# A hybrid gated-attention layer: three pairs of 256-column products made 512 columns wide, and the output's first product moved behind the last gate

## The chip, the cores and the metric

The kernel runs on one core of a Trainium2 chip. The metric is the device time of one execution in microseconds (us). Before the change the median of three runs is 765.3 us (764.86 to 766.08).

## The reference

One pre-norm layer on x of 1024 frames by 1024 columns, all float32:

```
h     = rmsnorm(x, norm_w)
parts = h @ w_in + b_in          # 1024 columns in; q, f, i, z of HGRN2; q, k, v, a, z of GLA; q, k, v, i, f, o, z of mLSTM
y_hg  = gated_head_norm(HGRN2(q, f, i), z)                # 4 heads, keys 128, values 128
y_gla = gated_head_norm(GLA(q, k, v, a), z)               # 4 heads, keys 64, values 128
y_ml  = gated_head_norm(mLSTM(silu(conv(q, k)), v, i, f) * sigmoid(o), z)   # 4 heads, keys 64, values 128
x     = x + concat(y_hg, y_gla, y_ml) @ w_out             # 1536 x 1024
out   = rmsnorm(x, final_norm_w)
```

Each branch is causal and worked out in chunks, with a state carried from one to the next. `gated_head_norm` normalises each head and multiplies by silu(z).

## The kernel before

**Products in three parts.** A float32 operand is split into a high and a low part of a shorter format (`whi`, `wlo` of weights; `HI[k]`, `LO[k]`, sixteen tiles named hT, of the normalised input, transposed). Each product of a block is three matmuls: high by high, high by low, low by high. `load_w` (L215 to 226) loads a raw weight tile of 128x1024 (`wraw`, two buffers, on SyncE's DMA queue), ScalarE copies the high part (L225), VectorE subtracts (L226). `whi` and `wlo` have three buffers each.

**Pieces.** The input projection is cut into pieces. An "nt" piece (`proj_nt`) holds 128 output columns as rows: two halves of 24 matmuls with 512 tokens. A "tn" piece (`proj_tn`, L354 to 376) holds tokens as rows: eight chunks of 128 tokens, each of 24 matmuls of 256 columns (L371 to 373), whose bank (`pm`, two in all) is then evacuated with scale and bias (`scaled`, L378). Tn pieces are the values of HGRN2 (v0, v1), of GLA (gv0, gv1), of mLSTM (mv0, mv1) and mLSTM's output gate (mo0, mo1); a tn piece of 256 columns holds two weight tiles.

**Order.** TensorE's order is that of the program text: `Weave` runs the pieces (`projections`, L908) as the main line and puts steps of attention chains between their triplets, by planned costs (0.65 for a triplet of 512 columns, 0.32 for one of 256), lags and free banks of PSUM (tags `pt`, `tp`, `po`, two banks each). The other engines' instructions are ordered by a scheduler, each engine in order; an instruction waits for its operands and buffers, and what stands behind it waits too. The order of the pieces in the last parts is, for r = 0 and 1: gq, gk, gv, two gz; then mq, mk, mv, mo, two mz.

**mLSTM's chain** (`ml_chain`, L806): convolution and silu of q and k (`conv`, L725 to 731), weights and attention matrices (`ml_att`, products L710, VectorE L711), states (`ml_states`), outputs (`ml_out`, L780). `ml_out` takes for each chunk a `po` bank, two or four small matmuls (L788, L790), and on ScalarE and VectorE the denominator (L792 to 794) and the gated output `osb` (L796), whose last read frees the bank. Then the head norm: squares on ScalarE (L525), the reciprocal root on GpSimd (`rstd_of`, L211 and L212), scaling (L528), transposes on TensorE (L533), the multiplication by silu(z) (L835).

**Sums.** `sum_steps` (L970 to 981) makes four sums of blocks of w_out for the output, through the two `wraw` buffers and back to DRAM, three steps each, between pieces.

**Output.** Behind all pieces seven products of 1536/2 x 512 blocks (a scheme that saves one of eight) of 72 matmuls each stand in program order (`product`, L1058 to 1068). The A operands are made of the y tiles by `a_form` (ScalarE L1040, VectorE L1041) after differences (`s2`, L1050 to 1052; `s1`, L1057), into hT tiles; the B operands by `b_form` (L1027 to 1029). y rows of HGRN2 and GLA are read back from DRAM. Product 1 (A11 by wq0) accumulates in four banks, is copied to P1 (L1117), and product 2 goes on adding in the same banks.

Of the kernel before, what the change touches and what calls it, by code (L numbers as in the profile page):

```python
# [45 lines left out]
PIECES = piece_columns()  # L46
WIDX, BIDX, VIDX = {}, {}, {}
NW = 0
for _n, _k, _c in PIECES:
# [82 lines left out]
def kernel(ctx: ExitStack, tc: tile.TileContext, x, xt, wt, wide, cols, vbias, wa2, wq, fw, masks, sel,  # L132
# [775 lines left out]
    def projections():  # L908
# [88 lines left out]

    with tc.manual_schedule(engines={mybir.EngineType.PE}):
        w.run(projections())

        nc.sync.dma_start(fwb, bass.AP(tensor=fw.tensor, offset=fw.offset, ap=[[0, 128], [1, D]]))
        for i in (0, 1, 2, 3):
            y_tile(i)
        for kh in range(2):
            for i in range(6):  # L1010
# [234 lines left out]
```

## Time and profile before

| | us |
|---|---|
| median of 3 runs | 765.3 (764.86 to 766.08) |
| profiled execution | 765.59 |
| its span on the core | 763.7 |
| TensorE busy | 747.7 (98%) |
| VectorE busy | 470.2 (62%) |
| ScalarE busy | 351.5 (46%) |
| GpSimd busy | 80.2 (11%) |

The mean granted clock of TensorE was 0.995 of full speed. The span runs from the first to the last instruction on the core; what lies around it is 1.9 us. Matmuls are pipelined, so a row of the trace overlaps the next, and the busy time is an upper bound on the work: how often matmuls start is read from the timeline. TensorE is the engine that sets the time; idle time on the others costs nothing in itself.

### The profile page before, as it was taken

The page shows a single profiled execution, that of the slowest core. Times are in us where ns is not written, and L with a number is a line of the kernel's source. Part 1 is how long each engine was busy: PE and PEld are TensorE (multiplying, and loading weights), DVE is VectorE, ACT ScalarE, POOL GpSimd, SP SyncE. Part 2 cuts the span into 40 slices and gives each one's busy share as a digit, 9 for nine tenths or more (in the row PEclk, how much of TensorE's full clock was granted, in tenths as well). Part 3 has the DMA queues.
Part 4 walks back from the last instruction along what each step waited for, and adds up shares of the span by engine and source line. Part 5 has one row for each costly group of instructions (what it writes and reads, how often), then busy time and mean ns, then how long its engine had stood idle before and what let it go on. Part 6 is the DMA issues. An engine that isn't in the chain of part 4 may idle for free.

```text
span 763.7 us, 14518 instructions
## 1 busy us (share of the span) xinstructions
PE 747.7 (98%) x5901; PEld 646.7 (85%) x5901; DVE 470.2 (62%) x998; ACT 351.5 (46%) x770; POOL 80.2 (11%) x107
## 2 busy tenths in 40 slices
PE   8999998999999999999999999999999999999996
PEld 6888886899887898788988889998899988878885
DVE  6896768676458447524753384543466258799863
ACT  6652669643453330554042661355252467264533
POOL 2000120010010020012000400001000112600011
PEclk9999999999999999999999999999999999999998
DMA  8331563031554041302021120122202067543323
GB/s 304 122 114 58 193 218 111 29 125 51 193 166 139 28 138 61 115 29 86 28 64 56 39 73 3 61 63 70 70 27 92 15 215 267 161 142 111 98 108 125
DMA packets 29826, 79.55 MB, mean 104 GB/s; under 512 B 3568, under 2 KB 7152, under 8 KB 29760
## 3 DMA queue, kind: packets, MB, share of 16 engines
q1 hardware_dynamic: 29088, 78.11, 31.0%
q8 instruction: 46, 0.75, 0.4%
q0 software_dynamic: 672, 0.53, 0.3%
q14 instruction: 20, 0.16, 0.1%
HBM read 62.69 MB, written 15.93 MB: 103 GB/s over the span
## 4 chain that ended last, share of the span: by engine, by line
PE 85%; DVE 6%; DMA 4%; ACT 2%; issue 2%; SPq 0%; POOL 0%; POOLq 0%; ACTq 0%; DVEq 0%
PE pm L339 11%; PE pm L341 11%; PE pm L340 11%; PE pm L371 8%; PE pm L372 8%; PE pm L373 8%; PE po L574 2%; PE po L576 2%; PE pt L489 2%; PE pt L559 1%; PE tp L533 1%; PE pt L458 1%; DMA wraw<-in_wt_dram 1%; PE tp L1067 1%; PE tp L1066 1%
## 5 line engine op out<-in xcount | busy, mean ns | idle before, releaser
L339 PE MATMUL pm<-hT,whi 128*128 128x512 f32 x400 | 163.0, 408 | 0.0
L341 PE MATMUL pm<-hT,wlo 128*128 128x512 f32 x400 | 157.1, 393 | 0.0
L340 PE MATMUL pm<-hT,whi 128*128 128x512 f32 x400 | 156.7, 392 | 0.0
L371 PE MATMUL pm<-whi,hT 128*128 128x256 f32 (+1 forms) x488 | 142.7, 292 | 0.0
L372 PE MATMUL pm<-wlo,hT 128*128 128x256 f32 (+1 forms) x488 | 138.4, 284 | 0.0
L373 PE MATMUL pm<-whi,hT 128*128 128x256 f32 (+1 forms) x488 | 138.3, 283 | 0.0
L371 PEld LDWEIGHTS pm<-whi,hT 128*128 128x128 f32 x488 | 93.2, 191 | 3.1 <-issue 2.2
L225 ACT ACTIVATE whi<-wraw 128x1024 fp32r<-128x1024 f32 (+4 forms) x47 | 45.6, 972 | 105.5 <-PE pm L373 55.8
L372 PEld LDWEIGHTS pm<-wlo,hT 128*128 128x128 f32 x488 | 93.3, 191 | 0.3
L373 PEld LDWEIGHTS pm<-whi,hT 128*128 128x128 f32 x488 | 93.2, 191 | 0.0
L341 PEld LDWEIGHTS pm<-hT,wlo 128*128 128x128 f32 x400 | 75.4, 188 | 16.6
L339 PEld LDWEIGHTS pm<-hT,whi 128*128 128x128 f32 x400 | 75.7, 189 | 16.2 <-issue 1.5
L340 PEld LDWEIGHTS pm<-hT,whi 128*128 128x128 f32 x400 | 75.8, 189 | 13.6
L226 DVE TENSOR_TENSOR wlo<-wraw,whi 128x1024 fp32r<-128x1024 f32 (+4 forms) x47 | 52.4, 1117 | 27.3 <-ACT whi L225 27.2
L378 DVE SCALAR_TENSOR_TENSOR big<-pm,rs,vb 128x256 f32<-128x256 f32 x72 | 32.2, 455 | 49.2 <-PE pm L373 49.1
L399 POOL COPY zg<-zg 128x1 f32<-128x1 f32 x12 | 21.7, 1810 | 219.2 <-ACT zg L397 219.2
L500 ACT ACTIVATE att<-dc 32x128 f32<-32x128 f32 (+1 forms) x48 | 16.5, 344 | 49.2 <-DVE dc L480 48.7
L211 POOL TENSOR_SCALAR st<-st 128x4 f32<-128x4 f32 x24 | 5.0, 207 | 268.6 <-ACT sq L525 268.6
L351 DVE TENSOR_TENSOR f<-pm,RSB 128x512 f32<-128x512 f32 x18 | 12.4, 688 | 30.9 <-PE pm L341 30.8
L397 ACT ACTIVATE zg<-zg,pc 128x512 f32<-128x512 f32 x24 | 17.2, 719 | 29.5 <-DVE zg L351 29.4
L525 ACT ACTIVATE sq<-po 128x128 f32<-128x128 f32 x64 | 17.8, 278 | 27.7 <-PE po L581 23.2
L351 DVE TENSOR_TENSOR zg<-pm,RSB 128x512 f32<-128x512 f32 x22 | 15.2, 691 | 23.1 <-PE pm L341 22.8
(396 smaller groups left out, 1458.2 us busy)
## 6 DMA issues: line engine op xcount, KB each, us to landing
wraw<-in_wt_dram SPq DMA_DIRECT2D x39, 512.0 KB, 3.9
wraw<-in_wq_dram SPq DMA_DIRECT2D x27, 512.0 KB, 3.6
wraw<-wsum SPq DMA_DIRECT2D x18, 512.0 KB, 3.5
wsum<-wraw SPq DMA_DIRECT2D x12, 512.0 KB, 2.9
big<-ydram SPq DMA_DIRECT2D x18, 256.0 KB, 5.4
big<-in_xt_dram SPq DMA_DIRECT2D x5, 512.0 KB, 5.7
ydram<-zg SPq DMA_DIRECT2D x8, 256.5 KB, 2.4
ydram<-zg SPq DMA_DIRECT2D x8, 255.5 KB, 3.3
```

The costliest lines, as they stand in the source:

```text
L225: nc.scalar.activation(hi[:, s], raw[:, s], AF.Copy)
L226: nc.vector.tensor_sub(lo[:, s], raw[:, s], hi[:, s].bitcast(F32))
L339: nc.tensor.matmul(p, hi[:, ks], HI[k][:, s], start=k == 0, stop=False)
L340: nc.tensor.matmul(p, hi[:, ks], LO[k][:, s], start=False, stop=False)
L341: nc.tensor.matmul(p, lo[:, ks], HI[k][:, s], start=False, stop=k == KC - 1)
L351: nc.vector.tensor_mul(dst(half), p, RSB[:, s])
L371: nc.tensor.matmul(p, HI[k][:, ts], hi[:, ks], start=k == 0, stop=False)
L372: nc.tensor.matmul(p, HI[k][:, ts], lo[:, ks], start=False, stop=False)
L373: nc.tensor.matmul(p, LO[k][:, ts], hi[:, ks], start=False, stop=k == KC - 1)
L378: nc.vector.scalar_tensor_tensor(dst, p, rs[:, c:c + 1], b, op0=OP.mult, op1=OP.add)
L399: nc.gpsimd.tensor_copy(z[:, 0:1], z[:, T:T + 1])
L525: nc.scalar.activation(sq, o[:, j, :], AF.Square, accum_out=st[:, j:j + 1])
```

## The change

The values of both GLA halves (gv0 and gv1), and for each r mLSTM's values and output gate (mv, mo), become one piece of 512 columns (`proj_tn2`: eight chunks of 24 matmuls, planned at 0.68 a triplet). It holds four weight tiles, so `whi` and `wlo` get four buffers. gv1 is thus made at r = 0; in its place at r = 1 stands mq0's projection, which before stood behind all gz. The values of a pair count as done with the gate's fourth chunk, and `ml_states`' second half waits for all gates, so `ml_out` moves from the mo piece into the mz pieces.

The output's first product becomes a last piece (`out_first`), woven with what is left of mLSTM's chain: it takes over the hT tiles, reads y2 to y5 of the first quarter early into four small tiles, makes both operands, takes four `pm` banks in turn and copies each to P1 (two tiles named al). Product 2 starts its own banks, and P1 is added to the result on VectorE (four additions). L numbers of the changed kernel are other ones: L339 to 341 become L344 to 346, L788 and L790 become L818 and L820, L796 becomes L826, L1041 becomes L1065.

```diff
-            hilo = [wp.tile([128, 1024], F32R, name=nm, bufs=3) for nm in ("whi", "wlo")]
+            hilo = [wp.tile([128, 1024], F32R, name=nm, bufs=4) for nm in ("whi", "wlo")]
...
+    def proj_tn2(names, evac):
+        vb = wk.tile([128, 512], F32, name="vb", bufs=1)
...
+        w = [load_w(wt[WIDX[names[0]] + a]) for a in range(4)]
+        for c in range(NC):
+            p = pmain.tile([128, 512], F32, name="pm")
+            ts = slice(c * 128, (c + 1) * 128)
+            for k in range(KC):
+                hi, lo = w[k // 2]
+                ks = slice(512 * (k % 2), 512 * (k % 2) + 512)
+                nc.tensor.matmul(p, HI[k][:, ts], hi[:, ks], start=k == 0, stop=False)
+                nc.tensor.matmul(p, HI[k][:, ts], lo[:, ks], start=False, stop=False)
+                nc.tensor.matmul(p, LO[k][:, ts], hi[:, ks], start=False, stop=k == KC - 1)
+                yield 0.68
+            for a in range(2):
+                evac[a](c, p[:, 256 * a:256 * a + 256], vb[:, 256 * a:256 * a + 256])
...
         yield from ml_states(r, K, E, V, S, 0)
+        yield lambda: len(gates) == NC
         yield from ml_states(r, K, E, V, S, 1)
+        states_of.append(r)
...
-            vs.append((yield from proj_v(f"gv{r}")))
+            if r == 0:
+                vv = [v_tile() for _ in range(2)]
+                yield from proj_tn2(PAIRS[0], [ev for _, ev in vv])
+                for a in range(2):
+                    gvs[a].append(vv[a][0])
+            else:
+                pq0.append((yield from proj_conv("mq0")))
...
-            V = yield from proj_v(f"mv{r}")
+            V, ev_v = v_tile()
...
                 gts.append(c)
-            yield from proj_tn(f"mo{r}", evo)
+                if c == 3:
+                    Vs.append(V)
+            yield from proj_tn2(PAIRS[1 + r], [ev_v, evo])
             for a in range(2):
                 zs.append((yield from proj_z(f"mz{2 * r + a}")))
+        yield from out_first()
...
+    def out_first():
+        yield lambda: len(states_of) > 1
...
+        load_y(0)
+        load_y(1)
+        tmp = [wk.tile([128, 768], F32, name="qm")[:, 0:512] for _ in range(2)] + [junk, wk.tile([128, 512], F32, name="kd")]
+        for i in range(2, 6):
+            nc.sync.dma_start(tmp[i - 2], ydram[i, :, 0:512])
+        b = b_form(wq[0])
+        a = a_form(lambda i: A11(i) if i < 2 else tmp[i - 2])
+        for c in range(4):
+            p = pmain.tile([128, 512], F32, name="pm")
+            yield from product(c, p, a, b, True, True)
+            nc.scalar.activation(P1[c], p, AF.Copy)
...
-        b1, a1 = b_form(wq[0]), a_form(A11)
-        pa = banks(tags_a)
...
-        for c in range(4):
-            product(c, pa[c], a1, b1, True, False, blocks=range(4))
-        for c in range(4):
-            product(c, pa[c], a1, b1, True, False, blocks=range(4, 6))
-            nc.scalar.activation(P1[:, c], pa[c], AF.Copy)
-        a2, b2 = a_form(A12), b_form(wq[2])
         for c in range(4):
-            product(c, pa[c], a2, b2, False, True)
+            nc.vector.tensor_add(xs(c, L), P1[c], xs(c, L))
+            run(c, pa[c], a2, b2, True, True)
```

How instructions stand now. First TensorE where mLSTM's last outputs begin their second pair of banks; `pm` is the last gate projection, `po` the outputs' banks. Before:

```order
L339 MATMUL pm_6433<-hT_113,whi_6428 128x512
L340 MATMUL pm_6433<-hT_114,whi_6428 128x512
L341 MATMUL pm_6433<-hT_113,wlo_6429 128x512
L788 MATMUL po_6482<-big_5785,att_95 128x129 [waits DVE_49,Activation_49]
L790 MATMUL po_6482<-S_6098,big_5804 128x129
L788 MATMUL po_6482<-big_5785,att_95 128x129
L790 MATMUL po_6482<-S_6098,big_5804 128x129
```

After, the same step (`po_5965` is the third bank, `po_5934` the first, whose place it takes):

```order
L344 MATMUL pm_5919<-hT_109,whi_5869 128x512
L345 MATMUL pm_5919<-hT_110,whi_5869 128x512
L346 MATMUL pm_5919<-hT_109,wlo_5870 128x512
L344 MATMUL pm_5919<-hT_111,whi_5869 128x512
L345 MATMUL pm_5919<-hT_112,whi_5869 128x512
L346 MATMUL pm_5919<-hT_111,wlo_5870 128x512
L818 MATMUL po_5965<-big_5383,att_95 128x129 [waits DVE_49,Activation_49]
L820 MATMUL po_5965<-S_5599,big_5417 128x129
L818 MATMUL po_5965<-big_5383,att_95 128x129
L820 MATMUL po_5965<-S_5599,big_5417 128x129
```

In both a third bank comes nine matmuls behind the second; after the change this stands in mz3's second half, before in mz2.

VectorE at that place, before: `osb` from the two banks, with what stands ahead.

```order
L793 TENSOR_TENSOR dn_6456<-dn_6456,mcol_123 128x2 [waits Activation_49]
L794 RECIPROCAL dn_6456<-dn_6456 128x2 [waits DVE_49]
L796 SCALAR_TENSOR_TENSOR osb_6449<-po_6451,dn_6456,big_6079 128x128 [waits DVE_49,PE_49]
L796 SCALAR_TENSOR_TENSOR osb_6450<-po_6451,dn_6456,big_6079 128x128
L793 TENSOR_TENSOR dn_6467<-dn_6467,mcol_123 128x2 [waits Activation_49]
L794 RECIPROCAL dn_6467<-dn_6467 128x2 [waits DVE_49]
L796 SCALAR_TENSOR_TENSOR osb_6449<-po_6462,dn_6467,big_6079 128x128 [waits DVE_49,PE_49]
L796 SCALAR_TENSOR_TENSOR osb_6450<-po_6462,dn_6467,big_6079 128x128
L1029 TENSOR_TENSOR al_6691<-wraw_6711,al_6690 128x1024 [waits DMAHW7_49,Activation_49]
L793 TENSOR_TENSOR dn_6487<-dn_6487,mcol_123 128x2 [waits Activation_49]
```

After: the last rows ahead of the first bank's `osb` (`hT` and `big` are operands of the output's products; the twelve rows ahead of these are nine more of the kind, two of two columns, and one product by a gate).

```order
L1065 TENSOR_TENSOR hT_6017<-dc_89,hT_6016 128x512 [waits PE_49,Activation_49]
L1065 TENSOR_TENSOR hT_6017<-kd_6050,hT_6016 128x512 [waits DMAHW6_49,Activation_49]
L1075 TENSOR_TENSOR qm_6330<-big_6043 128x512 [waits DVE_49]
L1065 TENSOR_TENSOR hT_6019<-big_6038,hT_6018 128x512 [waits PE_49,Activation_49]
L1065 TENSOR_TENSOR hT_6019<-big_6043,hT_6018 128x512 [waits DMAHW2_49,Activation_49]
L824 RECIPROCAL dn_5939<-dn_5939 128x2 [waits DVE_49]
L824 RECIPROCAL dn_5950<-dn_5950 128x2 [waits DVE_49]
L1076 TENSOR_TENSOR big_6038<-big_6038,qm_6324 128x512 [waits DVE_49]
L1076 TENSOR_TENSOR big_6043<-big_6043,qm_6330 128x512 [waits DVE_49]
L826 SCALAR_TENSOR_TENSOR osb_5932<-po_5934,dn_5939,big_5385 128x128 [waits DVE_49]
L826 SCALAR_TENSOR_TENSOR osb_5933<-po_5934,dn_5939,big_5385 128x128
```

The evacuations of the first bank (`osb` from `po_5934`) now stand behind operations of the output's operands, which in before came later.

SyncE's queue after GLA's values: before, `wraw` loads of pieces (in_wt), of the sums (wsum, in_wq) and the sum's store.

```order
L224 DMA wraw_3346<-in_wt_dram 128x1024 [waits DMAHW6_49,DVE_49]
L977 DMA wraw_3527<-wsum_479 128x1024 [waits DMAHW7_49,DMAHW1_49,DVE_49]
L978 DMA wraw_3528<-in_wq_dram 128x1024 [waits DMAHW2_49,DMAHW0_49,DVE_49]
L980 DMA wsum_479<-wraw_3527 128x1024 [waits DMAHW3_49,DVE_49]
L224 DMA wraw_3534<-in_wt_dram 128x1024 [waits DMAHW2_49]
L977 DMA wraw_3643<-wsum_479 128x1024 [waits DMAHW3_49]
L518 DMA ydram_122<-zg_2486 128x511 [waits DVE_49]
L515 DMA ydram_122<-zg_2486 128x513 [waits DVE_49,Pool_49]
L978 DMA wraw_3644<-in_wq_dram 128x1024 [waits DMAHW4_49,DVE_49]
L358 DMA vb_3907<-in_vbias_dram 128x256 [waits DMAHW1_49,DVE_49]
L980 DMA wsum_479<-wraw_3643 128x1024 [waits DVE_49]
L224 DMA wraw_3653<-in_wt_dram 128x1024 [waits DMAHW0_49]
```

After:

```order
L548 DMA ydram_122<-zg_2486 128x511 [waits DVE_49]
L545 DMA ydram_122<-zg_2486 128x513 [waits DVE_49,Pool_49]
L1115 DMA qm_6049<-ydram_122 128x512 [waits DMAHW7_49,DMAHW6_49,PE_49]
L1019 DMA wraw_3589<-in_wq_dram 128x1024 [waits DMAHW4_49,DVE_49]
L387 DMA vb_4586<-in_vbias_dram 128x256 [waits DVE_49]
L387 DMA vb_4586<-in_vbias_dram 128x256 [waits DMAHW3_49]
L1021 DMA wsum_479<-wraw_3588 128x1024 [waits DVE_49]
L229 DMA wraw_3604<-in_wt_dram 128x1024 [waits DMAHW5_49,DMAHW1_49]
L1018 DMA wraw_3665<-wsum_479 128x1024 [waits DMAHW4_49]
L1019 DMA wraw_3666<-in_wq_dram 128x1024 [waits DMAHW5_49,DVE_49]
L1021 DMA wsum_479<-wraw_3665 128x1024 [waits DMAHW0_49,DVE_49]
L229 DMA wraw_3675<-in_wt_dram 128x1024 [waits DMAHW7_49]
```

In both, steps of the sums and loads of pieces alternate; after the change one sum stands whole ahead of the load for gz1 (wraw_3604), and another between it and the load for gq1 (wraw_3675).

## Rows read from the trace of the kernel before

**Rows 1.** The page's first part: busy us of each engine, share of the span, instructions
```profile
PE 747.7 (98%) x5901; PEld 646.7 (85%) x5901; DVE 470.2 (62%) x998; ACT 351.5 (46%) x770; POOL 80.2 (11%) x107
```

**Rows 2.** Waits of TensorE: for whom, us in total, times, longest us
```profile
PE pt L429 <- ACT al L699: 2.0, 1, 2.0
...
PE pt L1068 <- DVE hT L1041: 1.3, 1, 1.3
...
PE pm L1066 <- DVE zg L1160: 0.6, 1, 0.6
```

**Rows 3.** Timeline of TensorE, 603 to 640: start us, us, engine, line, operation, tiles, form
```profile
604.62 0.28 PE L371 MATMUL pm<-whi,hT 128*128 128x256 f32 x1
...
604.98 0.28 PE L371 MATMUL pm<-whi,hT 128*128 128x256 f32 x1
...
637.74 0.39 PE L339 MATMUL pm<-hT,whi 128*128 128x512 f32 x1
...
639.10 0.39 PE L1066 MATMUL po<-whi,hT 128*128 128x512 f32 x1
```

**Rows 4.** Timeline of TensorE, 616 to 635, around mLSTM's last outputs
```profile
618.27 0.38 PE L788 MATMUL po<-big,att 128*128 128x129 f32 x2
...
619.97 0.48 PE L339 MATMUL pm<-hT,whi 128*128 128x512 f32 x1
...
633.85 0.60 PE L533 MATMUL tp<-ident,osb 128*128 128x128 f32 x4
634.20 0.48 PE L339 MATMUL pm<-hT,whi 128*128 128x512 f32 x1
```

**Rows 5.** Timeline of VectorE, 612 to 645
```profile
616.16 0.61 DVE L796 SCALAR_TENSOR_TENSOR osb<-po,dn,big 128x128 f32<-128x128 f32 x2
...
621.96 0.23 DVE L793 TENSOR_TENSOR dn<-dn,mcol 128x2 f32<-128x2 f32 x2
...
636.89 0.69 DVE L1050 TENSOR_TENSOR big<-big 128x512 f32<-128x512 f32 x1
...
642.92 0.69 DVE L351 TENSOR_TENSOR zg<-pm,RSB 128x512 f32<-128x512 f32 x1
```

**Rows 6.** Stretches: busy us of each engine, granted clock (PEclk), DMA share, GB/s
```profile
120.00:122.00 2.00, 0.55 (x2) 0.19 (x1) 2.00 (x11) 1.82 (x2) 0.00 (x0) 1.00 0.92 272
124.00:126.00 2.00, 2.00 (x13) 1.59 (x7) 2.00 (x8) 1.97 (x4) 0.00 (x0) 0.63 0.15 20
126.00:128.00 2.00, 2.00 (x7) 1.57 (x6) 1.62 (x8) 1.97 (x3) 0.36 (x1) 0.52 0.64 242
```

**Rows 7.** Groups by line and shape: busy us, mean ns of one | idle before, releaser
```profile
L225 ACT ACTIVATE whi<-wraw 128x1024 fp32r<-128x1024 f32 x39 | 41.2, 1058 | 100.6 <-PE pm L373 55.8 <-PE pm L340 37.5 <-DMA wraw<-in_wt_dram 5.9
...
L226 DVE TENSOR_TENSOR wlo<-wraw,whi 128x1024 fp32r<-128x1024 f32 x39 | 47.6, 1223 | 27.1 <-ACT whi L225 27.0
...
L979 DVE TENSOR_TENSOR wraw<-wraw 128x1024 f32<-128x1024 f32 x12 | 14.7, 1225 | 10.1 <-DMA wraw<-in_wq_dram 9.2 <-issue 0.8
```

**Rows 8.** Groups of VectorE by line and shape, convolution and mLSTM preparation
```profile
L511 DVE SCALAR_TENSOR_TENSOR zg<-tp,pc,zg 128x512 f32<-128x512 f32 x16 | 11.7, 746 | 4.4 <-PE tp L533 4.3
...
L730 DVE SCALAR_TENSOR_TENSOR f<-f,pc 128x1024 f32<-128x1024 f32 x6 | 7.7, 1280 | 0.1
...
L815 DVE TENSOR_SCALAR big<-al 64x1024 f32<-64x1024 f32 x4 | 2.7, 685 | 1.2 <-ACT al L731 1.1
...
L728 DVE TENSOR_SCALAR f<-f,pc 128x1024 f32<-128x1024 f32 x2 | 1.6, 807 | 0.0
```

**Rows 9.** The page's DMA issues: count, KB each, median us from issue to landing
```profile
wraw<-in_wt_dram SPq DMA_DIRECT2D x39, 512.0 KB, 3.9
wraw<-in_wq_dram SPq DMA_DIRECT2D x27, 512.0 KB, 3.6
...
wsum<-wraw SPq DMA_DIRECT2D x12, 512.0 KB, 2.9
```

**Rows 10.** Timeline of GpSimd, 640 to 670
```profile
644.42 17.01 POOL L399 COPY zg<-zg 128x1 f32<-128x1 f32 x1 [12.43 <-ACT zg L397]
```

More of the change, by code (lines that the diff above doesn't have):

```diff
@@ L46 @@
 PIECES = piece_columns()
+PAIRS = (("gv0", "gv1"), ("mv0", "mo0"), ("mv1", "mo1"))
+PAIRED = {n for p in PAIRS for n in p}
 WIDX, BIDX, VIDX = {}, {}, {}
@@ L58 @@
         VIDX[_n] = len(VIDX)
+for _p in PAIRS:
+    WIDX[_p[0]] = NW
+    NW += 4
 NB = len(BIDX)
@@ L996, in y_tile, with b_form, a_form @@
         return Y[i]
+    ASET, BSET, P1, made = [], [], [], [0, 0]
+    def b_form(src):
+        t = BSET[made[1] % 2]
+        made[1] += 1
+        for i in range(3):
+            raw = wp.tile([128, 1024], F32, name="wraw", bufs=2)
+            nc.sync.dma_start(raw, src[i])
+            nc.scalar.activation(t[2 * i], raw, AF.Copy)
+            nc.vector.tensor_sub(t[2 * i + 1], raw, t[2 * i].bitcast(F32))
+        return t
+    def a_form(src):
+        t = ASET[made[0] % 2]
+        made[0] += 1
+        for i in range(6):
+            s = slice(512 * (i % 2), 512 * (i % 2) + 512)
+            raw = src(i)
+            hi, lo = t[i // 2 * 2][:, s], t[i // 2 * 2 + 1][:, s]
+            nc.scalar.activation(hi, raw, AF.Copy)
+            nc.vector.tensor_sub(lo, raw, hi.bitcast(F32))
+        return t
@@ new lines, in product @@
+    def product(c, p, a, b, first, last, cols=slice(0, 512)):
+        for i in range(6):
+            ahi, alo = (a[i // 2 * 2 + q][:, 512 * (i % 2) + 128 * c:512 * (i % 2) + 128 * c + 128] for q in range(2))
+            bs = slice(512 * (i % 2) + cols.start, 512 * (i % 2) + cols.stop)
+            bhi, blo = (b[i // 2 * 2 + q][:, bs] for q in range(2))
+            nc.tensor.matmul(p[:, cols], ahi, bhi, start=first and i == 0, stop=False, skip_group_check=True)
+            nc.tensor.matmul(p[:, cols], ahi, blo, start=False, stop=False, skip_group_check=True)
+            nc.tensor.matmul(p[:, cols], alo, bhi, start=False, stop=last and i == 5, skip_group_check=True)
+            yield 0.69
@@ L1015 @@
-        hts = [ht.tile([128, 1024], F32R, name="hT") for _ in range(16)]
-        w0 = [wp.tile([128, 1024], F32R, name=nm, bufs=3) for _ in range(3) for nm in ("whi", "wlo")]
-        w0[4:4] = [fp.tile([128, 1024], F32R, name="al", bufs=2) for _ in range(2)]
-        ASET = [hts[0:6], hts[6:12]]
-        BSET = [w0[0:6], hts[12:16] + w0[6:8]]
-        made = [0, 0]
-        def b_form(src):
-            t = BSET[made[1] % 2]
-            made[1] += 1
-            for i in range(3):
-                raw = wp.tile([128, 1024], F32, name="wraw", bufs=2)
-                nc.sync.dma_start(raw, src[i])
-                nc.scalar.activation(t[2 * i], raw, AF.Copy)
-                nc.vector.tensor_sub(t[2 * i + 1], raw, t[2 * i].bitcast(F32))
-            return t
@@ L1070 @@
-        stats = const.tile([128, NC, 8], F32, name="stats")
+        for i in range(2, 6):
+            load_y(i)
         U2 = [wk.tile([128, 512], F32, name=nm) for nm in ("osb", "osb", "kd", "kd")]
@@ L1127 @@
         for c in range(4):
-            product(c, pb[c], a6, b6, True, False)
-            nc.vector.tensor_sub(U2[c], P1[:, c], pb[c])
+            run(c, pb[c], a6, b6, True, False)
+            nc.vector.tensor_sub(U2[c], P1[c], pb[c])
         a7, b7 = a_form(A11), b_form(wsum[2])
@@ L1185, in _layout @@
         vb[VIDX[name], :256] = b_in[c:c + 256]
+        if name in PAIRED:
+            continue
         for a in range(2):
@@ L1188, in _layout @@
                 wt[i + a] = kmajor(w_in[512 * a:512 * a + 512, c:c + 256])
+    first = {n: c for n, _, c in PIECES}
+    for pair in PAIRS:
+        both = np.concatenate([w_in[:, first[n]:first[n] + 256] for n in pair], axis=1)
+        for a in range(4):
+            wt[WIDX[pair[0]] + a] = kmajor(both[256 * a:256 * a + 256])
     cols[:, PC_NW:PC_NW + KC] = f("norm_w")[0].reshape(KC, 128).T
```

114 lines of the change are left out of this document (55 added, 59 removed).

## The prediction

> **What bounds the kernel now.** I read the busy shares first: TensorE (PE) is busy 747.7 of 763.7 us, so only 16 us of its span is idle [rows 1]. Then its table of waits: they are short and few; the longest is 2.0 us, and of the two in the output projection one is 1.3 us and one 0.6 us [rows 2]. So the time is TensorE's stream of matmuls, and two things can change it: fewer or cheaper matmuls, or new waits. Then the timeline of TensorE for the price of a matmul. Rows overlap there (a row of 0.39 us starts 0.23 us after the one before), so a price is the distance between starts: 0.36 us for three matmuls of 256 columns, 1.36 us for six of 512 [rows 3], that is 0.120 and 0.227 us once medians are taken over many rows. Last I read the queues of VectorE (DVE), ScalarE (ACT) and the loads around the places where the order of the changed kernel puts a wait.
>
> **The pairs.** Six pieces of 192 matmuls of 256 columns become three of 192 of 512. Per pair 384 x 0.120 = 46.1 us become 192 x 0.227 = 43.6 us; three times 2.5 us is 7.5 us less, all on TensorE's path. Nothing is multiplied less: two columns in one matmul cost 0.95 of what they cost in two. A matmul of 512 columns with weights and tokens in these places is not in the trace; the nearest row is the 512-column one of [rows 3], and I take it (bounds: 7 to 8 us saved).
> The Trainium skill, "TensorE: Matmul & The Clock Gate", back-to-back issue gap, gives columns / 2.4 GHz plus 2.5 ns for a matmul alone, 109 and 216 ns, by which the three pairs would save an estimated 1.2 us and the whole sum be 6 us worse. The trace has 120 ns for the small one, so here it disagrees, and the measured distances stand.
>
> **The wait ahead of product 1 (the largest term).** ml_out's second half needs two "po" banks again after 9 matmuls, and they are freed by VectorE's L826. In the order of before only operations of two columns stand ahead of the same step (L796), and TensorE's row at 618.27 follows its matmul without a wait [rows 4]. Now 17 operations on 128x512 tiles in SBUF (L1065, L1074, L1075, L1076, L1081, one L867) stand there, the operands of products 1 and 6. The same kinds of operations start 6.03/10 = 0.603 us apart (ten between the row at 636.89 and the one at 642.92) [rows 5]. Count from the start of mz3's second half, t = 0. VectorE cannot begin earlier than 0.7, since the evacuation of the first half stands ahead; the first hT pair is free after three matmuls (0.68) and one ScalarE copy of 0.6, so it begins at 1.35. Then 17 x 0.603 = 10.25, four operations of two columns at 0.1, and two L826 at 0.3 [rows 5]: the bank is free at 12.6. TensorE is there after 6 matmuls (1.36), four transposes (0.35), two banks of products (1.70) and 9 matmuls (2.04) [rows 3, 4]: 5.45. The wait is 7.15 us; I take 7.2 (bounds 6.5 to 8.5). Behind it stand mz3's last 9 matmuls and all of product 1. The last evacuation of mz3 shows in before how such a queue delays a step: it began at 642.92, 3.8 us after the last matmul had made way for the output's first at 639.10, harmless there as nobody wanted that bank [rows 3, 5].
>
> **What this wait draws after it.** A first matmul of the output waits for the evacuation of mz3's bank behind two operations fed by late loads, and a bank later for the copy of P1: 0.8 us (0 to 2). The clock: after the 2.0 us wait and its neighbours, in which TensorE was busy 0.55 of 2 us, the granted clock was 0.63 and 0.52 for 4 us, that is the lower level of 1.2 GHz for most of them, and that lost 0.37 x 2 + 0.48 x 2 = 1.7 us [rows 6]. A wait of 7 us is longer than any in the trace; I take 1.7 (0 to 1.7). On the other side the 1.3 us wait in product 6 and a neighbour of it go, since its operands are now made early: 1.5 us less (0 to 2.1). Product 2 no longer adds to product 1's bank; its four extra additions of 0.6 us on VectorE lie beside 72 matmuls of 16.3 us, and I cost them at nothing; without that cover they would be 2.4.
>
> **First halves of ml_out.** For both mLSTM pairs the two banks' L826 stand behind weight conversions of 1.2 us [rows 7]; TensorE comes 3 to 9 matmuls later: 0.5 us each, 1.0 together (0 to 1.6).
>
> **The start of the pair mv0, mo0.** mq0 and its convolution have moved forward, the k convolution now lies at the pair's start. TensorE's fourth attention product wants its bank while VectorE works through L758/L760 (0.81 + 3 x 1.28), two L845 (0.69 each) and two L541 (0.75 each) and evacuations [rows 8]; by the order the bank is free 11.6 us after the pair's first matmul, the operations above (8.0 us) and four evacuations and a conversion in front of them; TensorE is there after 36 matmuls (8.2), eight transposes (0.7) and two attention products (0.9): 9.8. With the next step 2.0 us (0 to 3.5).
>
> **The weights after the pair of GLA's values.** The pair holds all four weight tiles until its last chunk, and with four buffers the next piece's fourth slot comes free only 18 matmuls (4.1 us) before its end. From there everything is in series, because raw weights have two buffers and the sums wq + wq use the same two: conversion 1.06 and 1.2, addition 1.2 [rows 7], load 3.6, store 2.9, load of gz1 3.9 [rows 9], so 1.06 + 1.2 + 3.6 + 1.2 + 2.9 + 3.9 + 1.06 + 1.2 - 4.1 = 12.0 us after the pair's end; then once more 3.6 + 1.2 + 2.9 + 3.9 + 2.3 for gq1: 25.9. TensorE wants gz1 at 12.5 (48 matmuls of 0.227 are 10.9, with 1.6 of products between), in time, and gq1 at 23.4, too late by 2.5. With a little overlap of the steps I take 2.3 us (0 to 4). In before no wait of TensorE for whi or wlo stands among those of [rows 2]: the pieces there hold two of three buffers, which leaves one for the next piece.
>
> **Sum.** -7.5 - 1.5 + 7.2 + 0.8 + 1.7 + 1.0 + 2.0 + 2.3 = +6.0. The profiled execution took 765.6 us (span 763.7), so 771.6; it lay 0.3 above the median of 765.3, so I predict 771.3 us. Its own range is 767 to 776.
>
> **Rivals.**
> 1. GpSimd is starved. The last norm's rstd runs on GpSimd between VectorE's operations, and product 1's woven transposes wait for it. A copy of one column took 17.01 us while VectorE ran SBUF operations back to back [rows 10]. The Trainium skill, "SBUF — State Buffer", who interferes with whom, says that a VectorE instruction with two SBUF inputs and a GpSimd one that reads SBUF exclude each other for a whole instruction; the 17.01 us agrees. For it: ten such operations follow the last evacuation. Against it: they are fed by loads that start only then, which leaves gaps. Price: ten times 0.6, 6 us more: 777.
> 2. The waits only cancel the saving. The clock holds through the wait, and the two waits of some 2 us are slack: 771.3 - 1.7 - 2.3 - 2.0 = 765.3, no change. For it: each of them is a small difference of two sums of durations, and zero is inside its bounds. Against it: all three would have to fall out, and both chains are in series by the order.
> 3. The other side: the short waits are all slack. Everywhere but ahead of product 1 my arrival times differ by 0.1 to 3 us from the feeding engine's, on durations of another program. If VectorE is one or two operations earlier at each of these places, the three waits (5.3 us), the follow-up (0.8) and the clock (1.7) vanish and the sum is -7.5 - 1.5 + 7.2 = -1.8: 763.5, faster. It decides once the waits together fall below 9 us; with the wait for the po bank at its lower bound it is 762.8, and without it 756.
> 4. The change does not do what it says: the 512-column product here runs at a longer distance than 0.227. Each 0.01 us is 576 x 0.01 = 5.8 us. Rows speak against it; folded into the upper end.
>
> **Chances.** Forecast 0.54; rival 1 and 4 together 0.12; rival 2 0.13; rival 3 0.21. What a measurement can tell from no change is 0.2%, 1.5 us, so faster means under 763.8: 0.21, the same 0.13, slower 0.66. The range for 8 in 10 takes in rival 2, most of rival 3 and the lower part of rival 1: 760 to 778.
>
> **What would show it.** Right: matmuls of L395 to L397 0.227 us apart; VectorE's L1065, L1074 and L1081 in one unbroken run with L826 behind it; TensorE waiting about 7 us at L818 for osb of L826 just ahead of product 1, and a lower granted clock after it; some 2 us at L740 early in the first mLSTM pair; some 2 us for whi or wlo of L230/L231 at the first matmul of gq1; no wait in product 6. Wrong: a wait at L818 under 3 us; a transposition in product 1 that waits for GpSimd (rival 1); no waits at L740 and gq1 with the full clock (rival 3). A time under 763 would mean that I took program order on VectorE for lateness.

## The result, and the profile after

The changed kernel takes 777.09 us (median of 4 runs, 775.09 to 779.13), the kernel before in the same comparison 765.15 (4 runs, 764.86 to 766.08): ratio 1.0153, interval 1.0137 to 1.0168. It is slower, by 12 us where 6 were forecast. The profiled execution took 778.57 us, 13.0 more than that of before, so the rows below are of an execution 1.5 us above the median.

The page's first part, as [rows 1]:

```profile
PE 747.3 (96%) x5325; PEld 618.5 (80%) x5325; DVE 471.9 (61%) x1002; ACT 353.1 (45%) x772; POOL 63.2 (8%) x107
```

There are 576 matmuls fewer, 1152 of 256 columns having become 576 of 512, yet TensorE's busy time is nearly the same: slower clock (below) fills most of what was saved. Idle time rose from 16.0 to 29.5 us. Its waits, as [rows 2] (for whom, total, times, longest):

```profile
PE po L818 <- DVE osb L826: 6.8, 1, 6.8
PE pt L589 <- ACT kd L572: 3.4, 2, 3.2
PE pt L459 <- DVE f L467: 2.3, 1, 2.3
PE pt L488 <- DVE dc L464: 2.0, 2, 1.2
PE pt L740 <- DVE att L741: 1.6, 1, 1.6
...
PE po L818 <- DVE dn L824: 1.3, 2, 0.8
...
PE pm L1090 <- DVE zg L1215: 0.6, 1, 0.6
```

The first is the forecast's largest term; L740 is its start of the pair mv0/mo0, and L818 for dn its first halves of `ml_out`. The second was not forecast where it stands. The last is the 0.6 us at L1066 of [rows 2], neither more nor less, in both at the output's end. Product 6's wait for hT is gone.

Matmuls of a pair in the timeline of TensorE, in the form of [rows 3]:

```profile
458.20 0.39 PE L395 MATMUL pm<-whi,hT 128*128 128x512 f32 x1
458.43 0.39 PE L396 MATMUL pm<-wlo,hT 128*128 128x512 f32 x1
...
459.33 0.39 PE L397 MATMUL pm<-whi,hT 128*128 128x512 f32 x1
461.32 1.09 PE L740 MATMUL pt<-RX,sl 64*128 64x512 f32 x2 [1.60 <-DVE att L741]
```

They start 0.23 us apart (0.227 is the median of 549 distances), as the 512-column ones of [rows 3]. From 459.33 to 461.32 are 1.99 us, with the wait of 1.60 at L740 in it. VectorE at that place:

```profile
453.21 2.61 DVE L760 SCALAR_TENSOR_TENSOR f<-f,pc 128x1024 f32<-128x1024 f32 x2
...
458.72 1.28 DVE L760 SCALAR_TENSOR_TENSOR f<-f,pc 128x1024 f32<-128x1024 f32 x1
...
460.59 2.55 DVE L741 TENSOR_TENSOR att<-pt,neg 128x512 f32<-128x512 f32 x4
```

The k convolution and its follow-up stand ahead of L741, which frees the bank. Now the large wait, VectorE's timeline against [rows 5]:

```profile
636.63 1.29 DVE L1065 TENSOR_TENSOR hT<-big,hT 128x512 fp32r<-128x512 f32 x2 [0.35 <-PE pm L345]
...
645.95 1.27 DVE L1076 TENSOR_TENSOR big<-big,qm 128x512 f32<-128x512 f32 x2
647.14 1.12 DVE L826 SCALAR_TENSOR_TENSOR osb<-po,dn,big 128x128 f32<-128x128 f32 x4
```

and TensorE there, against [rows 4]:

```profile
640.74 0.39 PE L346 MATMUL pm<-hT,wlo 128*128 128x512 f32 x1
647.89 0.77 PE L818 MATMUL po<-big,att 128*128 128x129 f32 x2 [6.76 <-DVE osb L826]
```

After the first of these rows VectorE has no idle time up to 647.14: 10.5 us, nearly all of it operands of the output, and only then L826. On TensorE 640.74 and 647.89 lie 7.15 us apart, 6.76 of them idle. ScalarE at the wait that was not forecast there:

```profile
344.10 1.06 ACT L230 ACTIVATE whi<-wraw 128x1024 fp32r<-128x1024 f32 x1 [3.06 <-DMA wraw<-in_wt_dram]
...
350.18 1.06 ACT L230 ACTIVATE whi<-wraw 128x1024 fp32r<-128x1024 f32 x1 [2.39 <-DMA wraw<-in_wt_dram]
352.81 1.06 ACT L230 ACTIVATE whi<-wraw 128x1024 fp32r<-128x1024 f32 x1 [1.58 <-DMA wraw<-in_wt_dram]
...
354.38 0.57 ACT L572 ACTIVATE kd<-tp 128x512 f32<-128x512 f32 x1
```

gq1's weights came in time: the conversion of 344.10 is theirs, and TensorE stands at L589, just ahead of gq1, until 355.01. The copy kd that TensorE's L589 needs then stands behind conversions of the next pieces' weights, and these wait for late loads. Last, stretches behind the three waits as [rows 6] (busy us of each engine, then PEclk, DMA share, GB/s):

```profile
356.00:358.00 2.00, 2.00 (x13) 1.48 (x10) 0.90 (x3) 0.00 (x0) 0.00 (x0) 0.50 0.71 254
358.00:360.00 2.00, 2.00 (x6) 1.59 (x5) 0.50 (x2) 0.00 (x0) 0.00 (x0) 0.50 0.02 8
360.00:362.00 2.00, 2.00 (x8) 1.29 (x7) 0.00 (x0) 0.00 (x0) 0.00 (x0) 0.73 0.00 0
...
462.00:464.00 2.00, 2.00 (x7) 1.48 (x8) 1.14 (x2) 1.99 (x7) 0.00 (x0) 0.87 0.13 47
464.00:466.00 2.00, 2.00 (x5) 1.16 (x5) 0.00 (x0) 2.00 (x8) 0.00 (x0) 0.50 0.00 0
...
468.00:470.00 2.00, 2.00 (x6) 1.52 (x6) 0.88 (x2) 1.85 (x3) 0.00 (x0) 0.50 0.00 0
470.00:472.00 2.00, 2.00 (x10) 1.59 (x9) 0.00 (x0) 0.00 (x0) 0.00 (x0) 0.92 0.00 0
...
644.00:646.00 2.00, 0.00 (x0) 0.00 (x0) 2.00 (x7) 0.00 (x0) 0.00 (x0) 0.60 0.00 0
646.00:648.00 2.00, 0.11 (x1) 0.14 (x1) 2.00 (x7) 0.40 (x2) 0.00 (x0) 0.50 0.00 0
648.00:650.00 2.00, 2.00 (x10) 2.00 (x11) 0.26 (x1) 0.42 (x3) 0.00 (x0) 0.50 0.03 8
650.00:652.00 2.00, 2.00 (x11) 1.92 (x11) 1.66 (x6) 0.73 (x4) 0.00 (x0) 0.69 0.18 60
```

A PEclk of 0.50 is the lower level, 1.2 GHz; TensorE ran at it behind all three waits. With (1 - PEclk) x 2 us for each row in which it had work, the rows from 356 to 362 lose 2.5 us, those from 462 to 472 3.4 (three at 0.50), those from 648 to 652 1.6: 7.6 together.

What was found, by the waits' own times: -7.5 (pairs) - 1.5 (product 6) + 6.8 + 3.4 + 1.6 + 1.3 + 7.6 (clock) = 11.7, against 13.0 measured between the profiled executions. Of the rest, 2.6 are longer waits in earlier parts (L459 and L488: 2.3 + 1.2 + 2.0, in before 2.0 + 0.9 at L429, one row of 1.2 being below those shown), and 1.7 goes the other way, since the lower stretch of [rows 6] is not in this execution: 12.6.

### The profile page after: what moved, and what is told of

Its sections match the earlier page's. It is cut to its first block, busy times and chain, and to the rows that moved or that the text cites. A ratio compares the mean times of both kernels' runs of the same rounds, so it can differ in the third digit from the quotient of the medians.

```text
span 776.8 us, 13377 instructions
## 1 busy us (share of the span) xinstructions
PE 747.3 (96%) x5325; PEld 618.5 (80%) x5325; DVE 471.9 (61%) x1002; ACT 353.1 (45%) x772; POOL 63.2 (8%) x107
## 4 chain that ended last, share of the span: by engine, by line
PE 75%; DVE 8%; DMA 8%; ACT 6%; issue 2%; SPq 1%; POOLq 0%; DVEq 0%; POOL 0%; ACTq 0%
PE pm L344 10%; PE pm L346 9%; PE pm L345 9%; PE pm L395 5%; PE pm L396 5%; PE pm L397 5%; DMA wraw<-in_wt_dram 4%; DMA wraw<-in_wq_dram 2%; PE po L604 2%; ACT whi L230 2%; DVE wlo L231 2%; PE pm L376 1%; PE pm L1090 1%; PE pm L1092 1%; PE pm L1091 1%
## 5 line engine op out<-in xcount | busy, mean ns | idle before, releaser
L344 PE MATMUL pm<-hT,whi 128*128 128x512 f32 x400 | 163.5, 409 | 0.0
L344 PEld LDWEIGHTS pm<-hT,whi 128*128 128x128 f32 x400 | 75.7, 189 | 15.9 <-issue 1.3
L395 PE MATMUL pm<-whi,hT 128*128 128x512 f32 x192 | 78.7, 410 | 0.0
L396 PE MATMUL pm<-wlo,hT 128*128 128x512 f32 x192 | 75.9, 396 | 0.0
L397 PE MATMUL pm<-whi,hT 128*128 128x512 f32 x192 | 75.9, 395 | 0.0
L403 DVE SCALAR_TENSOR_TENSOR big<-pm,rs,vb 128x256 f32<-128x256 f32 x72 | 30.1, 454 | 57.6 <-PE pm L397 50.9
L395 PEld LDWEIGHTS pm<-whi,hT 128*128 128x128 f32 x192 | 36.6, 191 | 10.2 <-issue 2.9
L397 PEld LDWEIGHTS pm<-whi,hT 128*128 128x128 f32 x192 | 36.6, 191 | 8.0
L396 PEld LDWEIGHTS pm<-wlo,hT 128*128 128x128 f32 x192 | 36.7, 191 | 7.0
L1000 ACT ACTIVATE big<-big 128x256 f32<-128x256 f32 x16 | 6.7, 418 | 66.3 <-DVE big L403 66.3
L376 PE MATMUL pm<-whi,hT 128*128 128x256 f32 (+1 forms) x104 | 30.6, 294 | 0.0
L377 PE MATMUL pm<-wlo,hT 128*128 128x256 f32 (+1 forms) x104 | 29.8, 287 | 0.0
L378 PE MATMUL pm<-whi,hT 128*128 128x256 f32 (+1 forms) x104 | 29.8, 287 | 0.0
```

The lines of the kernel that those rows point to most:

```text
L344: nc.tensor.matmul(p, hi[:, ks], HI[k][:, s], start=k == 0, stop=False)
L376: nc.tensor.matmul(p, HI[k][:, ts], hi[:, ks], start=k == 0, stop=False)
L377: nc.tensor.matmul(p, HI[k][:, ts], lo[:, ks], start=False, stop=False)
L378: nc.tensor.matmul(p, LO[k][:, ts], hi[:, ks], start=False, stop=k == KC - 1)
L395: nc.tensor.matmul(p, HI[k][:, ts], hi[:, ks], start=k == 0, stop=False)
L396: nc.tensor.matmul(p, HI[k][:, ts], lo[:, ks], start=False, stop=False)
```

## The experiments

Ratios are to the kernel before, run on the same chip. Where an edit adds lines, the lines of its rows are shifted by some places.

**Which part costs what: three kernels with parts of the change.** `o_first_only` keeps the moved first product and all pieces at 256 columns. `gla_pair` is that with GLA's pair and mq0 moved. `ml_pairs` is that with the two mLSTM pairs alone.

```diff
-PAIRS = (("gv0", "gv1"), ("mv0", "mo0"), ("mv1", "mo1"))
+PAIRS = ()                               # o_first_only
+PAIRS = (("gv0", "gv1"),)                # gla_pair
+PAIRS = (("mv0", "mo0"), ("mv1", "mo1")) # ml_pairs
```

> Only the output's first product moved and woven; all six pieces of 256 columns, mq0 and gv1 in their old places (four buffers of weights stay). Theory: mLSTM's outputs end in mz2 again, so no bank waits behind the output's operands; the wait of 1.3 us in product 6 is gone: 763.7 (762.5 to 765.5). Rival (the moved product itself is what costs, wherever mLSTM's outputs lie): over 768.

> As o_first_only, and GLA's values as one piece of 512 columns (with mq0 moved forward); mLSTM's pieces at 256. Theory (the weights' chain after the pair takes back more than the pair saves): against o_first_only -2.5 by the matmuls, +3.3 by TensorE's wait for kd, whose copy stands on ScalarE behind conversions that wait for loads, +2 by the lower clock after it: +2.8, so 766.5 (765 to 768). Rival (that wait is a matter of the mLSTM pairs' loads behind it, and the pair gains its matmuls): 761.2.

> As o_first_only, and both mLSTM pairs at 512 columns; GLA's values at 256, gv1 and mq0 in their old places. Theory: against o_first_only -5.0 by the matmuls, +7 for the wait ahead of product 1 and +1 of lower clock, +1.6 in the first halves of mLSTM's outputs; the wait at the first pair's start is smaller, since the q convolution and not only the k one lies there or not at all: 0 to 4 with its clock; 768.5 to 773, 770 the middle. Rival (what is lost in the first pair comes from the pair itself and not from mq0's move): the wait for attention's bank there stays near 1.6 us with 3.5 us of lower clock, 773.

Measured: `o_first_only` 764.7 us (10 runs), 0.9988 (0.9979 to 0.9998); `gla_pair` 766.18 (10), 1.0009 (0.9997 to 1.0021); `ml_pairs` 770.48 (4), 1.0066 (1.0049 to 1.0082). All three near their expectations. The moved product alone has no wait at L818. With the mLSTM pairs added it is there:

```profile
PE po L818 <- DVE osb L826: 6.7, 1, 6.7
```

and no wait at L740. So the large wait comes with the mLSTM pairs, which shift `ml_out` into the last gate piece. That it takes the moved product too is read from what stands ahead of L826; no run has the pairs with the product in its old place. GLA's pair alone has already eaten its saving, in a shorter wait for kd and in 1.5 us of lower clock behind it (0.50 and 0.75 in the rows from 354 to 358):

```profile
PE pt L589 <- ACT kd L572: 2.4, 2, 2.1
```

The parts add up to 764.7 + 1.5 + 5.8 = 772.0. The remaining 5 us of the whole change appear only when both are in; what the traces show only there is the wait at L740 with the 3.4 us of clock behind it, and kd's wait grown from 2.1 to 3.2. Part of it is chance, since one wait does not cost the same clock in every execution (`mq0_back`, next).

**The wait at L740: `mq0_back`** puts mq0's projection back into its old place.

```diff
-            else:
-                pq0.append((yield from proj_conv("mq0")))
...
-                PQK.append(pq0[0] if nm == "q" and not r else (yield from proj_conv(f"m{nm}{r}")))
+                PQK.append((yield from proj_conv(f"m{nm}{r}")))
```

> The changed kernel with mq0's projection and convolution back behind all gz, gv1 still paired with gv0 (so nothing stands in gv1's old place at r = 1). Theory (the wait for attention's bank at the first mLSTM pair comes of the k convolution that mq0's move leaves at its start): that wait of 1.6 us and its stretch of lower clock (3.5 us) go: 777.6 - 5 = 772.5, more if GLA's second chain waits for lack of a piece beside it. Rival (the wait belongs to the pair, which starts attention at once): wait and clock stay, 777 to 778.

775.47 us (4), 1.0133 (1.0112 to 1.0155). The wait at L740 stays at 1.6 us, so mq0's move is not its cause: the rival was right there. The time came out between the two by kd's wait and by the clock: behind kd's wait, now 2.1 us, the clock stayed full, where `gla_pair` lost 1.5 us behind one just as long, and behind L740 the rows lose 1.7 us instead of 3.4.

```profile
356.00:358.00 2.00, 2.00 (x11) 1.60 (x10) 1.07 (x4) 0.00 (x0) 0.00 (x0) 1.00 0.59 229
```

With `ml_pairs`, which lacks the wait at L740, this says that it takes GLA's pair and mLSTM's together. A new wait of 1.2 us for S at L611 appeared.

**The kd wait: `sums_later`** makes two steps of the w_out sums that ran between the GLA pieces run in the second GLA part.

```diff
-                next(sums, None)
+                if r:
+                    next(sums, None)
```

> The changed kernel with the two sums of output weights that stood between gz0, gz1 and gq1 put off to the second GLA part. Theory (TensorE's 3.2 us wait for kd: ScalarE's copy stands behind conversions that wait for loads, which the sums' loads and store delay in two raw buffers): that wait and the 2 us of lower clock behind it go: 777.6 - 5 = 772.5 (771.5 to 774.5). Rival (four held weight tiles alone make the loads late): the wait keeps over 2 us, 776 to 778.

772.68 us (4), 1.009 (1.0073 to 1.0107), as expected: kd's longest wait went from 3.2 to 0.4 us, and 4.4 us came back. This shows that the sums are the cause. That they delay the weights by holding the raw buffers and the load queue is read from the order of the loads. The wait cost more than its own length: with it went the lower clock behind it, 1.00 now in every row from 350 to 364.

**The clock: `fill`** adds 14, 7 and 28 matmuls with a zero operand in the three waits, into the bank that is open there.

```diff
+            nc.tensor.matmul(cur[0], zz, HI[KC - 1][:, 0:512], start=False, stop=False, skip_group_check=True)
...
+            fill(14)   # ahead of L589
...
+            fill(7)    # ahead of L740
...
+            fill(28)   # ahead of L818
```

> The changed kernel with matmuls by a tile of zeros added into a running sum in three of TensorE's waits: 14 ahead of the attention product that waits for kd (3.2 us), 7 ahead of the attention bank's wait at the first mLSTM pair (1.6 us), 28 ahead of the po bank (6.8 us). The sums stay as they are. Theory (after each wait the granted clock stands at the lower level for some us, since TensorE was idle): the waits shrink to nothing, TensorE passes the places at the same time as before, and the lower level goes: -2.0 - 3.5 - 1.0 = 771.1 us (770.5 to 773). Rival (the lower level has another cause, or is costless): 777 to 778, with the granted clock at 0.985 still.

772.5 us (4), 1.0092 (1.0077 to 1.0107), mean clock 0.998 against 0.985. The other engines' work is not changed; TensorE only does useless work while it waits. A stretch in the place of one above, where the clock was 0.50:

```profile
464.00:466.00 2.00, 2.00 (x10) 1.67 (x9) 0.88 (x2) 2.00 (x6) 0.00 (x0) 1.00 0.00 0
```

So 4.6 of the 12 us are lower clock behind waits, by medians (777.09 - 772.5), and 6.4 by profiled executions (778.57 - 772.15).

**Can the large wait be ordered away? Five tries.** `hold` queues the VectorE operations of the A operands behind the last L826. `hold2` does so with product 1's alone and queues the rest behind the last norm. `hold3` queues product 2's behind the last norm, and product 6's and all later ones behind the second of the three splits of product 2's weights, which was meant to be the order in which TensorE wants them.

```diff
+        with tc.issue_after(osb_last[0].ins):      # hold
+            return a_form_(src)
...
+        with tc.issue_after((osb_last if made[0] == 0 else gate)[0].ins):      # hold2
+            return a_form_(src)
...
+        with tc.issue_after((osb_last[0] if n == 0 else gate[0] if n == 1 else b2_last[0]).ins):   # hold3
+            return a_form_(src)
```

> The changed kernel, with VectorE's operations of the output's operands (splits and differences) queued behind the last evacuation of mLSTM's outputs, nothing else. Theory (VectorE's queue makes the wait): no wait of TensorE for osb ahead of product 1, no lower clock there, at most 1 to 2 us of short waits inside product 1; 777.1 - 7 - 1 + 1.5 = 770.5 us (769 to 772). Rival (the work of VectorE is only moved, and product 1 then waits for its operands as long as the bank did): a wait of 5 us or more inside product 1, 775 to 777.

> As hold, but only the splits of product 1's A operand follow the last evacuation; all later operands (the differences, the splits of products 2 to 7, their B operands) are queued on VectorE behind one small operation that reads the last norm's reciprocal root, so that VectorE leaves GpSimd its gap. Theory (in hold GpSimd's 0.19 us step took 8.61 us beside an unbroken run of two-input operations in SBUF, and the transposes waited for it): no wait at the transposes, no wait at the po bank, under 1 us for hT; 779.7 - 5.7 - 1.4 - 2.0 of lower clock = 770.6 us (769 to 772.5). Rival (the transposes' wait comes of ScalarE's queue or the loads): the wait of 5 us stays, 778 or more.

> As hold2, with VectorE's operands in the order in which TensorE wants them: product 1's splits behind the last evacuation, product 2's behind the small operation that reads the last norm's reciprocal root, and everything of product 6 and later behind the second split of product 2's weights. Theory (what lies between the po bank and product 2 is a matter of order on VectorE, as it has 16 us of product 1 for it): no wait over 1 us from product 1 to 6 and the full clock there: 778.7 - 5.1 - 4 = 769.6 us (768.5 to 771.5). Rival (VectorE has more to do from mz3's second half to product 6 than time, since mLSTM's outputs moved there; order only moves the wait): waits of 4 us or more in products 1, 2 or 6, 774 or more.

`hold` 779.74 us (4), 1.0178 (1.0144 to 1.0211); `hold2` 778.7 (4), 1.0175 (1.0155 to 1.0195); `hold3` 781.99 (4), 1.022 (1.0192 to 1.0248). My expectation failed all three times; each time the wait at L818 for osb went and came back elsewhere. In `hold`, TensorE's transposes waited for the last norm, whose step on GpSimd stood still:

```profile
PE tp L563 <- ACT osb L558: 5.7, 1, 5.7
...
654.38 8.61 POOL L216 TENSOR_SCALAR st<-st 128x4 f32<-128x4 f32 x1 [4.58 <-ACT sq L555]
```

The step ends at 662.99, as VectorE's gapless run of two-input operations ends with this row:

```profile
662.25 0.68 DVE L1080 TENSOR_TENSOR big<-big,qm 128x512 f32<-128x512 f32 x1
```

In the changed kernel the same step took 0.19 us. This is the mechanism of the prediction's first rival, though not in the kernel it was named for. The Trainium skill, "SBUF — State Buffer", who interferes with whom, calls the port that the two engines share an exclusive lock, held for a whole instruction; the 8.61 us agree with that blocking, and here it lasted over thirteen VectorE operations on end. In `hold2` the step is back at 0.19 us, but product 2 waits:

```profile
PE po L1106 <- DVE hT L1064: 3.1, 1, 3.1
...
PE po L1106 <- DVE wlo L1064: 2.0, 1, 2.0
```

and in `hold3` products 6 and 2:

```profile
PE pt L1111 <- DVE hT L1084: 5.3, 2, 3.2
PE po L1110 <- DVE wlo L1065: 3.7, 1, 3.7
```

`mend` is `hold3` with `sums_later`, and the first k convolution queued behind the attention products' L741:

```diff
+        if not r:
+            with tc.issue_after(att_last[0].ins):
+                conv(PQK[1], 2 + r, K)
```

> As hold3, with the two sums put off (sums_later), and at r = 0 the k convolution queued on VectorE behind the four attention evacuations of L741. Theory (the three places are apart): 769.6 - 5 (kd and its clock) - 1.6 - 3 (attention's bank and its clock) = 760 us (759 to 763), faster than before by some 5 and than o_first_only by 4, so that all of the pairs' 7.5 us but 3 comes through. Rival (k convolution then makes mLSTM's chain late, or the waits move on): 765 or more.

776.38 us (4), 1.0147 (1.0126 to 1.0168). The waits for kd and at L740 are gone, and the output's first product starts at 635.0 us (changed kernel 653.4, before 639.1). But from its first matmul to its last the output then takes 132.8 us, against 117.6 in before and 116.6 in the changed kernel:

```profile
653.00:663.00 10.00, 5.89 (x23) 4.53 (x22) 10.00 (x17) 3.75 (x5) 0.00 (x0) 0.92 0.57 206
663.00:673.00 10.00, 10.00 (x41) 8.12 (x40) 10.00 (x16) 5.36 (x10) 0.00 (x0) 0.91 0.40 120
673.00:683.00 10.00, 5.86 (x26) 4.50 (x24) 10.00 (x18) 8.05 (x14) 0.00 (x0) 0.95 0.35 106
```

VectorE is busy 30 of 30 us, TensorE has 8.25 us idle: by these rows VectorE's amount of work has become the limit here. `hold3_light` tests that. It is `hold3` without the 18 differences of product 6's A operand, so products 3, 6 and 7 take other operands and the output differs.

```diff
-        t = wk.tile([128, 768], F32, name="qm")[:, 0:512]
-        nc.vector.tensor_sub(A11(i), A21(i), A11(i))
-        nc.vector.tensor_sub(t, A22(i), A11(i))
-        nc.vector.tensor_sub(A12(i), A12(i), t)
-        return t
+        return A22(i)
```

> As hold3, but the 18 differences that make product 6's A operand (and change products 7 and 3 with it) are left out, some 10.8 us of VectorE's work. Theory that has taken the first one's place (from mz3's second half to product 6 VectorE has more work than TensorE has matmuls, 46 us to 42 by mend's rows; order only moves the wait): TensorE's waits of 3.7 us in product 2 and 5.3 in product 6 shrink to under 2 together, and with 4 us or so of lower clock 782.0 falls to 768 to 771. Rival (the waits come of the loads of weights in series through two raw buffers, not of VectorE's work): waits of 3 us or more in products 2 and 6 stay, 777 or more.

777.36 us (4), 1.015 (1.0129 to 1.017), 4.6 less than `hold3`; by the time the rival was right. Product 6's wait is gone, so that one was VectorE's amount of work. Product 2's stays:

```profile
PE po L1106 <- DVE wlo L1065: 4.2, 1, 4.2
```

Timeline of ScalarE and VectorE there, for product 2's third weight tile:

```profile
665.30 1.06 ACT L1064 ACTIVATE whi<-wraw 128x1024 fp32r<-128x1024 f32 x1 [3.96 <-DMA wraw<-in_wq_dram]
...
663.23 3.10 DVE L1096 TENSOR_TENSOR big<-big 128x512 f32<-128x512 f32 x5
...
666.85 2.49 DVE L1084 TENSOR_TENSOR hT<-big,hT 128x512 fp32r<-128x512 f32 x4
...
669.86 1.22 DVE L1065 TENSOR_TENSOR wlo<-wraw,whi 128x1024 fp32r<-128x1024 f32 x1
```

The load (issued at 661.60, once a raw buffer was free) is late, and TensorE waits 1.4 us for whi. But whi is done at 666.36, and VectorE comes to the split only at 669.86: for 3.5 us operands of later products stand ahead of it. So most of the 4.2 us is VectorE's queue again, and the rival's loads explain the smaller part. `hold3` has the same: whi done at 662.06, the split at 666.25, a wait of 3.7 us. Its order named the second split, not the third; no run queues the later operands behind the third.

**A version that keeps a gain: `gla_sums`** is `gla_pair` and `sums_later` together.

```diff
+PAIRS = (("gv0", "gv1"),)
...
+                if r:
+                    next(sums, None)
```

> As gla_pair (product 1 moved, GLA's values at 512 columns, mLSTM's pieces at 256), with the two sums put off. Theory (one pair's 2.5 us come through once its wait for kd, 2.1 us, and 0.9 us of lower clock are gone, and the last stretch keeps the old place of mLSTM's outputs): 766.2 - 3 = 763.2 us on the scale where before is 766.0, that is 0.996 of before and some 1.5 us under o_first_only. Rival (the put-off sums make a wait in the second GLA part): 765 to 767, ratio 1.0.

764.81 us (12 runs, 763.83 to 771.68), 1.0005 (0.9985 to 1.0025): not told apart from before, and not the gain expected. The kd wait is gone, and one of 0.8 us took its place:

```profile
PE po L611 <- DVE S L595: 0.8, 1, 0.8
```

Three of the twelve runs took 769.1 to 771.7 us at mean clocks of 0.992 to 0.996, as the others have them (0.992 to 0.998); what made them longer is open. No version beat the kernel before by more than the 0.12% of `o_first_only`.

## Why the prediction was right, and where it was mis-sized

- **The direction and the large wait: right.** 7.2 us forecast at L818, 6.8 found, with the 17 operations it counted in one unbroken run in front. `ml_pairs` and `o_first_only` show that it needs the mLSTM pairs, `hold` that it is those operations: queued behind L826 they leave no such wait. But the prediction took it for a matter of order. Each of the three orders tried left TensorE waiting for an operand that VectorE came to late, or for GpSimd beside it; whether another order would do is open.
- **The size: short by half.** 777.1 lies 1.1 us above the forecast's own range of 767 to 776 and inside the wider one of 760 to 778. It is also the time that rival 1 gives (777), by luck: what rival 1 describes is not in the changed kernel (below).
- **The pairs: right.** 0.227 us a matmul, so -7.5; rival 4 is out. Product 6's wait is gone as forecast, and `o_first_only` is 1.3 us under before by medians, 0.9 by its ratio (0.2 to 1.6), where 1.5 stood.
- **The start of mv0/mo0: right in place and size** (2.0 forecast, 1.6 found; TensorE was there 10.1 us after the pair's first matmul and went on at 11.7, where 9.8 and 11.6 stood). That the k convolution ahead of L741 makes it, `mend` bears out: with it queued behind, the wait is gone. That mq0's move put it there is refuted by `mq0_back`; why it takes both kinds of pairs stays open.
- **First halves of `ml_out`: right,** 1.0 forecast, 1.3 found; it was L824 behind the other work, not L826.
- **"The weights after the pair of GLA's values": right cause, wrong victim.** The chain of sums, stores and loads does delay (`sums_later`), but gq1's weights were split 22.5 us after the pair's end, not 25.9, and TensorE reached gq1 later than the 23.4 forecast. The late loads held up ScalarE, and with it kd: 3.4 us where 2.3 stood for whi or wlo.
- **"What this wait draws after it": the step that was mis-sized.** "I take 1.7 (0 to 1.7)" priced one stretch of lower clock, behind the long wait. There were three, worth 4.6 us by `fill` and 7.6 by rows of the profiled execution. The long one cost 1.6, as forecast; the waits at L589 and L740, behind which no clock was put down, cost 2.5 and 3.4 in that execution. The 0.8 us of followers did not come: no wait of the changed kernel is for mz3's evacuation or for the copy of P1. Term by term, found less forecast: clock +5.9, kd +1.1, L818 -0.4, L740 -0.4, first halves +0.3, followers -0.8, together +5.7, which brings 6.0 to the 11.7 found.
- **Rivals 2 and 3 fell:** the clock did not hold, and the waits at L818 and L740 came in the forecast's size. Only the wait for gq1's weights was slack, and a longer one stood at kd. **Rival 1** did not happen in the changed kernel, where GpSimd is quick, the copy of [rows 10] included:

```profile
654.64 0.19 POOL L216 TENSOR_SCALAR st<-st 128x4 f32<-128x4 f32 x1 [21.58 <-ACT sq L555]
...
658.67 0.73 POOL L429 COPY zg<-zg 128x1 f32<-128x1 f32 x1 [0.69 <-ACT zg L427]
```

## What to carry to other kernels

A saving of a few us on an engine that is 98% busy lasts only while nothing else is made late: before widening a piece, count what the move brings together on the other engines, and look for what frees each bank, behind which queue. Price a wait on TensorE as its length plus a stretch at the lower clock behind it, which cost nothing to 5.1 us behind waits of about 2 us here. When reordering only moves the wait to the next product, look which operation stands ahead of the one wanted, and count the engine's work in that stretch.

## What was unexpected of the hardware

- A longer wait did not cost more clock. In the changed kernel, behind the waits of 1.6 and 3.2 us the granted clock was 0.50 for four us and more of work; the one of 6.8 us saw the clock at 0.60 and 0.50 while TensorE still stood, and it was back 4 us after work began.
- The same wait did not cost the same clock. Behind the 1.60 us at L740 the rows lose 1.7 us in `mq0_back` and in `sums_later`, 3.4 in the changed kernel and 5.1 in `hold`, whose clock is low from 459 to 471:

```profile
465.00:467.00 2.00, 2.00 (x5) 1.43 (x5) 0.03 (x1) 1.98 (x3) 0.00 (x0) 0.50 0.00 0
```

- Waits do not always bring it. In the stretch of [rows 6] the changed kernel's profile shows TensorE just as idle, and the clock stays full:

```profile
120.00:122.00 2.00, 0.67 (x3) 0.19 (x1) 2.00 (x11) 1.98 (x3) 0.00 (x0) 1.00 0.00 0
...
124.00:126.00 2.00, 2.00 (x10) 1.62 (x10) 2.00 (x7) 1.98 (x4) 0.00 (x0) 1.00 0.00 0
```

  Before shows 0.63 and 0.52 there. Of the fourteen profiles here eight show the lower clock in that stretch and six do not: `sums_later`, whose edit acts only later, has 0.50 there, the changed kernel 1.00. The four executions of the changed kernel have mean clocks of 0.985 to 0.990 and 775.1 to 779.1 us. What decides is left open. The Trainium skill, "TensorE: Matmul & The Clock Gate", Part 1, calls the number of slow matmuls at a kernel's start run-variable; these runs show the like in the middle.
- Useless matmuls with zeros in a wait kept the clock at 0.998 and gave back 4.6 us.
- A GpSimd step on 128x4 elements took 8.61 us instead of 0.19 beside a run of VectorE operations with two SBUF inputs.
